# Up projection: a couple's second product added onto the bank of its first, and one weight split moved from GpSimd to VectorE

## The chip, the cores and the metric

The kernel runs on one core of a Trainium2 chip. The metric is the device time of one execution in microseconds (us), the median of several runs. The core has TensorE (PE in the rows; PEld is its loading of weights), VectorE (DVE), ScalarE (ACT), GpSimd (POOL) and SyncE (SP), which issues the transfers. Each engine executes its instructions in order and waits where a semaphore is not there yet.

## The reference

One layer of a bidirectional encoder on 2048 positions of width 1024, in float32: two token mixers, a merge, and a channel mixer. Only the channel mixer matters here:

```
h2 = _rmsnorm(x, norm2_g[l])
u = h2 @ ffn_up[l]
...
u = cw[0] * _shift_prev(u) + cw[1] * u + cw[2] * _shift_next(u) + ffn_conv_b[l]
u_gate, u_val = jnp.split(u, 2, axis=-1)
x = x + (jax.nn.silu(u_gate) * u_val) @ ffn_down[l]
```

## The kernel before

**Float32 from three products.** Each float32 operand is split into a high part (a cast by ScalarE, names ending in h) and a low part (source minus high, names ending in l; both in `split`, L226 and L227). A product is high·high, high·low and low·high, 4 blocks of the contraction each: 12 matmuls of 128x512 into one bank of TensorE's accumulator memory (PSUM).

**Seven products for eight.** The up projection, L1501 to L1680, works on pairs: one tile of 128 gate features (`ug`) and one of 128 value features (`uv`), over two blocks of 512 positions at a time. That is a 2x2 block product, done with Winograd's seven products: weights A11, S2, S3, S1, A12, A22, S4 against activations B11, T2, T3, T1, B21, T4, B22, in this order in `up_pair`. A11 and A12 are `whi`/`wlo`, S1 and S2 are `s1h`/`s1l`, S3 and A22 are `s3h`/`s3l`, S4 is `s4h`/`s4l`. So a pair is 84 matmuls, and the rows name a product by its activations: "mT3h,s3l" is the last third of S3·T3.

**What is made of the products.** The four results are `c11`, `c12` (halves of `ug`) and `c21`, `c22` (halves of `uv`). Before the change ScalarE copies the first product out of its bank (L1639), and seven additions by VectorE (`plus`, L1506) bring in the others; each product has a bank of its own, from a ring of eight (`bank`).

**The rest of a pair.** Two rows of weights are loaded by SyncE into `rw` (`raw_tile`, four buffers). GpSimd forms the sums (L1561), four additions a pair. ScalarE casts the high parts; the low parts are subtracted by GpSimd (`wlo`, `s3l`) and VectorE (`s1l`, `s4l`). The split weights S1, S3, S4 have one buffer each, so they are made anew as soon as the pair before is through with them. Then the convolution (`conv`): ScalarE makes the middle tap (L1605), VectorE adds the two others (L1606, L1607), twice for `ug` and twice for `uv`; ScalarE takes the SiLU (L1613), VectorE multiplies (L1615), SyncE writes the result out. GpSimd copies the edge columns (`halo`).

**Order.** There are two sweeps q of 21 pairs each, over the position blocks 1 and 2, then 0 and 3. At the turn between them all seven activation matrices are replaced (`load_mat`): half of each passes through one buffer, `wraw`, the next transfer into which waits for VectorE's subtraction from the last. A scheduler sets the order on each engine from priorities; `plus` has a raised one. Behind the second sweep a last tile of 128 mixed features and then the down projection (L1714 to L1716) follow.

Of the kernel before, what the change touches and what calls it, by code (L numbers as in the profile page):

```python
# [166 lines left out]
def _body(tc, A, out, dump=None, upto=99):  # L167
    nc = tc.nc
# [4 lines left out]
    def pool(stack, name, bufs=1, space=None, **kw):  # L173
        if space is None:
            return stack.enter_context(tc.tile_pool(name=name, bufs=bufs, **kw))
        return stack.enter_context(tc.tile_pool(name=name, bufs=bufs, space=space, **kw))
# [48 lines left out]
    def split(hi, lo, src, lo_eng=None, hi_eng=None):  # L225
        (hi_eng or nc.scalar.copy)(out=hi, in_=src)  # L226
        (lo_eng or nc.vector).tensor_tensor(out=lo, in0=src, in1=hi.bitcast(F32), op=ALU.subtract)  # L227
# [70 lines left out]
    def operand(b, q, **kw):  # L298
        t = [[q.tile([128, 4, BT], F32R, name=f"h{nm}{b}{i}", **kw) for nm in ("hi", "lo")] for i in range(2)]
        return [Halves([x[j] for x in t]) for j in range(2)]  # L300
# [3 lines left out]
    for b in range(NB):  # L304
        x_, y_ = operand(b, hb, **FOP) if b == NB - 1 else operand(b, hp)
# [93 lines left out]
    for b in range(NB):  # L399
        ps = pg.tile([128, 512], F32, name="pg", tag="pg")  # L400
# [3 lines left out]
        o = ev.tile([128, 512], F32, name="ev", tag="ev")  # L404
# [1015 lines left out]
    mats = {}  # L1420
# [77 lines left out]
    def prod(ps, *terms):  # L1498
        mm = [(w[ph == 2][:, k, :], x[ph == 1][:, k, :]) for w, x in terms for ph in range(3) for k in range(4)]
        for i, (w_, x_) in enumerate(mm):  # L1500
            nc.tensor.matmul(ps, w_, x_, start=i == 0, stop=i == len(mm) - 1)  # L1501
        return ps

    def plus(o, ps, t):
        with tc.high_priority(300):
            nc.vector.tensor_tensor(out=o, in0=ps, in1=t, op=ALU.add)  # L1506
# [29 lines left out]
    fw = pool(s6, "fw", reuse_waits="tile")  # L1536
# [6 lines left out]
    def raw_tile(src):  # L1543
        r = fr.tile([128, 8, 128], F32, name="rw", tag="rw", bufs=4)
        if src is not None:
            sync.dma_start(out=f2(r), in_=src)
        return r
# [10 lines left out]
    def pair_weights(i):  # L1558
        r1, r2 = raw_tile(A["wup"][2 * i]), raw_tile(A["wup"][2 * i + 1])
        a, b = slice(0, 4), slice(4, 8)  # L1560
        ps_ = lambda o, x, y, op: nc.gpsimd.tensor_tensor(out=o, in0=x, in1=y, op=op)  # L1561

        def parts(q, names, src, eng, n=8):
            h, l = [q.tile([128, n, 128], F32R, name=x, tag=x, bufs=2 if q is wp else 1) for x in names]
            split(f2(h), f2(l), f2(src), lo_eng=eng)
            return h, l

        h, l = parts(wp, ("whi", "wlo"), r1, nc.gpsimd)
        w = {"A11": (h[:, a], l[:, a]), "A12": (h[:, b], l[:, b])}
        rs = raw_tile(None)  # L1570
        ps_(rs[:, a], r2[:, a], r2[:, b], ALU.add)
        ps_(rs[:, b], rs[:, a], r1[:, a], ALU.subtract)
        h, l = parts(fw, ("s1h", "s1l"), rs, nc.vector)
        w["S1"], w["S2"] = (h[:, a], l[:, a]), (h[:, b], l[:, b])
        ps_(r2[:, a], r1[:, a], r2[:, a], ALU.subtract)
        h, l = parts(fw, ("s3h", "s3l"), r2, nc.gpsimd)
        w["S3"], w["A22"] = (h[:, a], l[:, a]), (h[:, b], l[:, b])
        ps_(r1[:, b], r1[:, b], rs[:, b], ALU.subtract)
        w["S4"] = parts(fw, ("s4h", "s4l"), r1[:, b], nc.vector, 4)
        return w  # L1580

    def bank():
        nbank[0] += 1
        return pus[(nbank[0] - 1) % 8 >= 3].tile([128, 512], F32, name="pu", tag="pu")
# [5 lines left out]
    def u_tile(q, m, tag):  # L1590
        u = fu.tile([128, 1030], F32, name=tag, tag=tag, bufs=2)
        if q == 1:
            nc.gpsimd.memset(u[:, 0:1], 0.0)
            nc.gpsimd.tensor_copy(out=u[:, 513:517], in_=halo[:, m, :])
            nc.gpsimd.memset(u[:, 1029:1030], 0.0)
        return u

    def u_done(q, m, u):
        if q == 0:
            nc.gpsimd.tensor_copy(out=halo[:, m, 0:2], in_=u[:, 2:4])  # L1600
            nc.gpsimd.tensor_copy(out=halo[:, m, 2:4], in_=u[:, 1024:1026])
# [8 lines left out]
    def glu(q, i, ug, uv):  # L1610
        for c0, n, t0 in SEG[q]:
            g = conv(2 * i, ug, c0, n)
            nc.scalar.activation(out=g, in_=g, func=AF.Silu)  # L1613
            v = conv(2 * i + 1, uv, c0, n)
            nc.vector.tensor_tensor(out=v, in0=v, in1=g, op=ALU.mult)  # L1615
            sync.dma_start(out=d_act[i, :, t0:t0 + n], in_=v)
# [11 lines left out]
    def up_pair(q, i, w, after):  # L1628
        ug, uv = u_tile(q, 2 * i, "ug"), u_tile(q, 2 * i + 1, "uv")
        c11, c12, c21, c22 = [u[:, c] for u in (ug, uv) for c in COLS[q]]  # L1630

        def pr(a, b):
            ps = prod(bank(), (w[a], mats[b]))
            after(b)
            return ps

        p1 = pr("A11", "B11")
        with tc.high_priority(300):
            nc.scalar.copy(out=c11, in_=p1)  # L1639
        plus(c12, pr("S2", "T2"), c11)  # L1640
        plus(c21, pr("S3", "T3"), c12)
        p5 = pr("S1", "T1")
        plus(c12, p5, c12)
        plus(c22, p5, c21)
        plus(c11, pr("A12", "B21"), c11)
        plus(c21, pr("A22", "T4"), c21)
        plus(c12, pr("S4", "B22"), c12)
        u_done(q, 2 * i, ug)
        u_done(q, 2 * i + 1, uv)
        return lambda: glu(q, i, ug, uv)  # L1650
# [9 lines left out]

    steps = [(0, 21)] + [(q, i) for q in range(2) for i in range(21)] + [(1, 21)]
    weights = lambda i: load_w(A["wup"][42]) if i == 21 else pair_weights(i)
    nw, pend = None, None
    for n, (q, i) in enumerate(steps):
        w = nw
        if n + 1 < len(steps):
            nw = weights(steps[n + 1][1])
        if n == 0:
            load_mat("T4", 7)
        turn = q == 0 and i == 20  # L1670
        if i == 21:
            fin = mixed(q, w)
        else:
            fin = up_pair(q, i, w, lambda b: load_mat(b, MATS.index(b)) if turn else None)
        if pend:
            pend()
        pend = fin
# [43 lines left out]
    def banks(tt):  # L1721
        return [pd.tile([128, 512], F32, name=f"pd{tt % 4}{i}", tag=f"pd{tt % 4}{i}") for i in range(2)]
# [59 lines left out]
    for w, (tt, k0) in enumerate(work):  # L1782
        ah, al = nx
        if k0 == 0:
            ps = banks(tt)
# [41 lines left out]
```

## Time and profile before

| | |
|---|---|
| median of 3 runs | 3567.59 us (3567.49 to 3571.24) |
| the profiled execution: its own time | 3570.72 us |
| its span, first to last instruction | 3568.9 us |
| TensorE busy | 3280.0 us, 92% |
| VectorE busy | 2328.1 us, 65% |
| ScalarE busy | 1571.5 us, 44% |
| GpSimd busy | 957.1 us, 27% |
| up projection, from its first to its last matmul | about 2200 to 3074 us |

The shares are averages over stages with different limits. Rows of the time line give the start, the duration, the engine, the line, what is written and what is read, the number of instructions, and in brackets how long the engine stood idle before and for whom.

### The profile page before, as it was taken

The numbers are of one execution on the slowest core, as the hardware profiler recorded it, in microseconds if no ns is written. First come the engines' busy times: TensorE is split into PE (matmuls) and PEld (weight loads), VectorE is DVE, ScalarE is ACT, GpSimd is POOL, SyncE is SP. The second block draws the span as 40 slices with busy tenths as digits, with TensorE's granted clock in tenths as the row PEclk, the third lists the DMA queues.
The fourth block names the chain that finished last, engine by engine and source line by source line (L and its number), as shares of the span: only waits on it lengthen the run. The fifth ranks groups of instructions, "written<-read, shape, count | busy, mean of one in ns | idle before, by whom it ended". The sixth has DMA issues, their size and how long they took to land.

```text
span 3568.9 us, 58167 instructions
## 1 busy us (share of the span) xinstructions
PE 3280.0 (92%) x22232; PEld 2612.0 (73%) x22232; DVE 2328.1 (65%) x3945; ACT 1571.5 (44%) x2870; POOL 957.1 (27%) x757
## 2 busy tenths in 40 slices
PE   7999999999978888888768999999989999999998
PEld 6787778766656766766656788877768777878887
DVE  5207664587865666666776467989899998723222
ACT  4214443455546776676544333344444434411111
POOL 1122222134440000000003314676676666100000
PEclk9999999999989999998889999999989999999999
DMA  4233443688874565556889656222232222523222
GB/s 148 93 118 107 132 137 129 193 225 228 230 227 152 161 188 155 181 181 195 238 241 340 220 160 197 83 77 80 80 130 89 81 79 77 177 81 114 84 84 62
DMA packets 403222, 531.29 MB, mean 149 GB/s; under 512 B 61504, under 2 KB 250560, under 8 KB 402944
## 3 DMA queue, kind: packets, MB, share of 16 engines
q1 hardware_dynamic: 402944, 527.58, 47.5%
q8 instruction: 175, 2.87, 0.3%
q14 instruction: 103, 0.84, 0.1%
HBM read 345.02 MB, written 181.93 MB: 148 GB/s over the span
## 4 chain that ended last, share of the span: by engine, by line
PE 32%; DVE 22%; issue 6%; DMA 6%; ACT 5%; POOL 1%; SPq 1%; DVEq 0%; ACTq 0%; POOLq 0%
PE pg L241 7%; PE pu L1501 6%; PE pd L1714 4%; PE pd L1715 4%; PE pd L1716 4%; DVE cv L1606 3%; PE pf L1218 2%; DVE ug L1506 2%; DVE s1l L227 2%; DVE uv L1506 2%; DVE tm L924 1%; DVE XX L925 1%; DMA d_m<-ev 1%; POOL s3l L227 1%; DVE cv L1607 1%
## 5 line engine op out<-in xcount | busy, mean ns | idle before, releaser
L227 POOL TENSOR_TENSOR wlo<-wraw,whi 128x1024 fp32r<-128x1024 f32 x46 | 115.2, 2504 | 1166.6 <-ACT whi L226 924.2
L1561 POOL TENSOR_TENSOR rw<-rw 128x512 f32<-128x512 f32 x168 | 274.5, 1653 | 4.4 <-DVE cv L1606 1.1
L1714 PE MATMUL pd<-wdh,whi 128*128 128x512 f32 x672 | 261.6, 391 | 1.3 <-DVE ug L1506 1.3
L1715 PE MATMUL pd<-wdl,whi 128*128 128x512 f32 x672 | 261.4, 389 | 0.0
L1716 PE MATMUL pd<-wdh,wlo 128*128 128x512 f32 x672 | 259.3, 389 | 0.0
L1218 PE MATMUL pf<-fop,whi 128*128 128x512 f32 x576 | 175.7, 442 | 87.4 <-ACT whi L226 59.4
L241 PE MATMUL pg<-hlo,whi 128*128 128x512 f32 x928 | 251.9, 404 | 0.0
L241 PE MATMUL pg<-hhi,whi 128*128 128x512 f32 x928 | 248.8, 403 | 3.1 <-ACT whi L226 3.1
L241 PE MATMUL pg<-hhi,wlo 128*128 128x512 f32 x928 | 247.2, 401 | 0.0
L241 PEld LDWEIGHTS pg<-hhi,whi 128*128 128x128 f32 x928 | 175.8, 192 | 55.8 <-issue 15.6
L241 PEld LDWEIGHTS pg<-hlo,whi 128*128 128x128 f32 x928 | 175.2, 192 | 52.7 <-issue 17.5
L241 PEld LDWEIGHTS pg<-hhi,wlo 128*128 128x128 f32 x928 | 175.1, 191 | 50.4 <-issue 14.7
L1218 PEld LDWEIGHTS pf<-fop,whi 128*128 128x128 f32 x576 | 112.7, 207 | 124.0 <-ACT whi L226 65.5
L1605 ACT ACTIVATE cv<-ug,vec 128x511 f32<-128x511 f32 (+1 forms) x88 | 71.9, 817 | 250.3 <-DVE ug L1506 250.3
L226 ACT CAST whi<-wraw 128x1024 fp32r<-128x1024 f32 x114 | 119.4, 1048 | 109.0 <-PE pg L241 53.7
L1703 ACT CAST whi<-wraw 128x1024 fp32r<-128x1024 f32 (+1 forms) x36 | 35.3, 980 | 265.8 <-PE pd L1715 185.9
L1606 DVE SCALAR_TENSOR_TENSOR cv<-ug,vec,cv 128x511 f32<-128x511 f32 (+1 forms) x88 | 125.4, 1425 | 36.8 <-ACT cv L1605 36.8
L1714 PEld LDWEIGHTS pd<-wdh,whi 128*128 128x128 f32 x672 | 126.1, 188 | 30.4 <-issue 4.7
L1716 PEld LDWEIGHTS pd<-wdh,wlo 128*128 128x128 f32 x672 | 126.1, 188 | 26.2
L1715 PEld LDWEIGHTS pd<-wdl,whi 128*128 128x128 f32 x672 | 126.1, 188 | 25.6
L1613 ACT ACTIVATE cv<-cv 128x511 f32<-128x511 f32 (+1 forms) x84 | 52.9, 630 | 198.4 <-DVE cv L1607 198.4
L1706 DVE TENSOR_TENSOR wlo<-wraw,whi 128x1024 fp32r<-128x1024 f32 (+1 forms) x36 | 39.3, 1092 | 150.5 <-ACT whi L1703 150.5
(470 smaller groups left out, 8230.4 us busy)
## 6 DMA issues: line engine op xcount, KB each, us to landing
rw<-wup SPq DMA_DIRECT2D x84, 512.0 KB, 3.5
wraw<-win SPq DMA_DIRECT2D x74, 512.0 KB, 4.2
Lt<-d_lt SPq DMA_DIRECT2D x64, 512.0 KB, 5.2
d_lt<-arbk SPq DMA_DIRECT2D x96, 256.0 KB, 3.9
d_gate<-ev SPq DMA_DIRECT2D x64, 256.0 KB, 3.6
X<-d_vt SPq DMA_DIRECT2D x64, 256.0 KB, 4.4
bj<-d_lt SPq DMA_DIRECT2D x128, 128.0 KB, 3.7
d_m<-ev SPq DMA_DIRECT2D x64, 256.0 KB, 5.1
```

The costliest lines, as they stand in the source:

```text
L226: (hi_eng or nc.scalar.copy)(out=hi, in_=src)
L227: (lo_eng or nc.vector).tensor_tensor(out=lo, in0=src, in1=hi.bitcast(F32), op=ALU.subtract)
L241: nc.tensor.matmul(ps, (wh, wh, wl)[ph], (xh, xl, xh)[ph], start=(ph == 0 and i == 0), stop=(ph == 2 and i == n - 1))
L1218: nc.tensor.matmul(ps, (wh, wh, wl)[ph][:, k0 + k, :], (hi, lo, hi)[ph][:, k, :], start=i == first[u] and k == 0, stop=i == last[u] and k ...
L1501: nc.tensor.matmul(ps, w_, x_, start=i == 0, stop=i == len(mm) - 1)
L1506: nc.vector.tensor_tensor(out=o, in0=ps, in1=t, op=ALU.add)
L1561: ps_ = lambda o, x, y, op: nc.gpsimd.tensor_tensor(out=o, in0=x, in1=y, op=op)
L1605: nc.scalar.activation(out=c, in_=u[:, c0:c0 + n], func=AF.Identity, scale=vc("cw1", m), bias=vc("cb", m))
L1606: nc.vector.scalar_tensor_tensor(out=c, in0=u[:, c0 - 1:c0 - 1 + n], scalar=vc("cw0", m), in1=c, op0=ALU.mult, op1=ALU.add)
L1714: nc.tensor.matmul(ps, a, wdh[k][:, cs], start=(k == 0), stop=False)
L1715: nc.tensor.matmul(ps, a, wdl[k][:, cs], start=False, stop=False)
L1716: nc.tensor.matmul(ps, l, wdh[k][:, cs], start=False, stop=False)
```

## The change

Three of the seven products are no longer put into a bank of their own. A12·B21 is added onto the bank of A11·B11, A22·T4 onto that of S3·T3, S4·B22 onto that of S1·T1, after the first product of the couple has been read out of it. So a pair takes four banks, VectorE makes five additions instead of seven, and ScalarE two copies (`taken`) instead of one. `s3l` goes from GpSimd to VectorE.

```diff
-        h, l = parts(fw, ("s3h", "s3l"), r2, nc.gpsimd)
+        h, l = parts(fw, ("s3h", "s3l"), r2, nc.vector)
...
-        def pr(a, b):
-            ps = prod(bank(), (w[a], mats[b]))
+        def pr(a, b, ps=None):
+            first = ps is None
+            ps = bank() if first else ps
+            mm = [(w[a][ph == 2][:, k, :], mats[b][ph == 1][:, k, :]) for ph in range(3) for k in range(4)]
+            for n, (w_, x_) in enumerate(mm):
+                nc.tensor.matmul(ps, w_, x_, start=first and n == 0, stop=n == len(mm) - 1, skip_group_check=True)
             after(b)
             return ps
+        def taken(o, ps):
+            with tc.high_priority(300):
+                nc.scalar.copy(out=o, in_=ps)
         p1 = pr("A11", "B11")
-        with tc.high_priority(300):
-            nc.scalar.copy(out=c11, in_=p1)
+        taken(c11, p1)
         plus(c12, pr("S2", "T2"), c11)
-        plus(c21, pr("S3", "T3"), c12)
+        p3 = pr("S3", "T3")
+        plus(c22, p3, c12)
         p5 = pr("S1", "T1")
-        plus(c12, p5, c12)
-        plus(c22, p5, c21)
-        plus(c11, pr("A12", "B21"), c11)
-        plus(c21, pr("A22", "T4"), c21)
-        plus(c12, pr("S4", "B22"), c12)
+        plus(c22, p5, c22)
+        taken(c11, pr("A12", "B21", p1))
+        plus(c21, pr("A22", "T4", p3), c12)
+        plus(c12, pr("S4", "B22", p5), c12)
```

The matmuls of a steady pair keep their order on TensorE. On VectorE, from the addition of S2·T2 in one pair of the first sweep on, this stood before (the additions in turn: S2·T2, S3·T3, S1·T1 twice, then behind `s1l` A12·B21, A22·T4, S4·B22):

```order
L1506 TENSOR_TENSOR ug<-pu,ug 128x512 [waits PE_49,Activation_49]
L1615 TENSOR_TENSOR cv<-cv 128x511 [waits DVE_49,Activation_49]
L1506 TENSOR_TENSOR uv<-pu,ug 128x512 [waits DVE_49,PE_49]
L1506 TENSOR_TENSOR ug<-pu,ug 128x512 [waits DVE_49,PE_49]
L1506 TENSOR_TENSOR uv<-pu,uv 128x512
L227 TENSOR_TENSOR s1l<-rw,s1h 128x1024 [waits Activation_49]
L1506 TENSOR_TENSOR ug<-pu,ug 128x512 [waits PE_49]
L1606 SCALAR_TENSOR_TENSOR cv<-ug,vec,cv 128x511 [waits Activation_49]
L1506 TENSOR_TENSOR uv<-pu,uv 128x512 [waits PE_49]
L1606 SCALAR_TENSOR_TENSOR cv<-uv,vec,cv 128x511 [waits DMAHW7_49,Activation_49]
L1607 SCALAR_TENSOR_TENSOR cv<-uv,vec,cv 128x511 [waits DVE_49]
L1506 TENSOR_TENSOR ug<-pu,ug 128x512 [waits PE_49]
```

And this stands there now (the additions: S2·T2, S3·T3, S1·T1, then A22·T4 and S4·B22):

```order
L1506 TENSOR_TENSOR ug<-pu,ug 128x512 [waits PE_49]
L1615 TENSOR_TENSOR cv<-cv 128x511 [waits DVE_49,Activation_49]
L1506 TENSOR_TENSOR uv<-pu,ug 128x512 [waits DVE_49,PE_49]
L1506 TENSOR_TENSOR uv<-pu,uv 128x512 [waits DVE_49,PE_49]
L227 TENSOR_TENSOR s1l<-rw,s1h 128x1024 [waits Activation_49]
L1606 SCALAR_TENSOR_TENSOR cv<-ug,vec,cv 128x511 [waits Activation_49]
L1506 TENSOR_TENSOR uv<-pu,ug 128x512 [waits PE_49]
L227 TENSOR_TENSOR s3l<-rw,s3h 128x1024 [waits DMAHW0_49,Activation_49]
L1606 SCALAR_TENSOR_TENSOR cv<-uv,vec,cv 128x511 [waits DMAHW7_49,Activation_49]
L1607 SCALAR_TENSOR_TENSOR cv<-uv,vec,cv 128x511 [waits DVE_49]
L1506 TENSOR_TENSOR ug<-pu,ug 128x512 [waits PE_49]
L227 TENSOR_TENSOR s4l<-rw,s4h 128x512 [waits DMAHW5_49,Activation_49]
```

One addition of S1·T1 and the one of A12·B21 are gone, and `s3l` has come in between the addition of A22·T4 and the convolution of `uv` that reads its result.

On ScalarE, from the middle tap of the second half on, this stood before (the COPY is the first product's):

```order
L1605 ACTIVATE cv<-ug,vec 128x511 [waits DVE_49,Activation_49]
L1605 ACTIVATE cv<-uv,vec 128x511 [waits DMAHW2_49]
L1613 ACTIVATE cv<-cv 128x511 [waits DVE_49]
L1639 COPY ug<-pu 128x512 [waits PE_49]
L1613 ACTIVATE cv<-cv 128x511 [waits DVE_49]
L226 CAST s1h<-rw 128x1024 [waits PE_49,Activation_49,Pool_49]
L226 CAST whi<-rw 128x1024 [waits DMAHW5_49,PE_49]
L1605 ACTIVATE cv<-ug,vec 128x511 [waits DVE_49]
L226 CAST s3h<-rw 128x1024 [waits PE_49,DMAHW4_49,Activation_49,Pool_49]
```

And this stands there now; behind `whi` the second COPY takes A11·B11 + A12·B21 out of the bank:

```order
L1605 ACTIVATE cv<-ug,vec 128x511 [waits DVE_49]
L1605 ACTIVATE cv<-uv,vec 128x511 [waits DMAHW2_49]
L1644 COPY ug<-pu 128x512 [waits PE_49]
L1613 ACTIVATE cv<-cv 128x511 [waits DVE_49] x2
L226 CAST s1h<-rw 128x1024 [waits PE_49,Pool_49]
L226 CAST whi<-rw 128x1024 [waits DMAHW5_49,PE_49]
L1644 COPY ug<-pu 128x512 [waits DVE_49,PE_49,Activation_49]
L1605 ACTIVATE cv<-ug,vec 128x511 [waits Activation_49]
L226 CAST s3h<-rw 128x1024 [waits DMAHW4_49,PE_49,Pool_49]
```

The middle tap of `ug` ahead of `s3h` waited for an addition of VectorE, and now waits for the copy on its own engine.

At the turn, on VectorE, between the splits of two matrices that pass through `wraw`, this stood before:

```order
L227 TENSOR_TENSOR mT3l<-wraw,mT3h 128x1024 [waits DMAHW4_49,Activation_49]
L227 TENSOR_TENSOR mT1l<-ev,mT1h 128x512 [waits DMAHW5_49,Activation_49]
L1506 TENSOR_TENSOR uv<-pu,uv 128x512 [waits DVE_49,PE_49]
L1606 SCALAR_TENSOR_TENSOR cv<-ug,vec,cv 128x511 [waits Activation_49]
L1506 TENSOR_TENSOR ug<-pu,ug 128x512 [waits PE_49]
L1606 SCALAR_TENSOR_TENSOR cv<-uv,vec,cv 128x511 [waits DMAHW3_49,Activation_49]
L227 TENSOR_TENSOR s4l<-rw,s4h 128x512 [waits DMAHW1_49,Activation_49]
L1607 SCALAR_TENSOR_TENSOR cv<-ug,vec,cv 128x511 [waits DVE_49]
L227 TENSOR_TENSOR mB21l<-ev,mB21h 128x512 [waits DMAHW0_49,Activation_49]
L1607 SCALAR_TENSOR_TENSOR cv<-uv,vec,cv 128x511 [waits DVE_49]
L1606 SCALAR_TENSOR_TENSOR cv<-ug,vec,cv 128x511 [waits Activation_49]
L227 TENSOR_TENSOR mT1l<-wraw,mT1h 128x1024 [waits DMAHW1_49,Activation_49]
```

And this stands there now:

```order
L227 TENSOR_TENSOR mT3l<-wraw,mT3h 128x1024 [waits DMAHW4_49,Activation_49]
L1606 SCALAR_TENSOR_TENSOR cv<-ug,vec,cv 128x511 [waits Activation_49]
L227 TENSOR_TENSOR mT1l<-ev,mT1h 128x512 [waits DMAHW5_49,Activation_49]
L1506 TENSOR_TENSOR uv<-pu,ug 128x512 [waits PE_49]
L227 TENSOR_TENSOR s3l<-rw,s3h 128x1024 [waits Activation_49]
L227 TENSOR_TENSOR mB21l<-ev,mB21h 128x512 [waits DMAHW0_49,Activation_49]
L1606 SCALAR_TENSOR_TENSOR cv<-uv,vec,cv 128x511 [waits DMAHW3_49,Activation_49]
L1506 TENSOR_TENSOR ug<-pu,ug 128x512 [waits PE_49]
L227 TENSOR_TENSOR s4l<-rw,s4h 128x512 [waits DMAHW1_49,Activation_49]
L227 TENSOR_TENSOR mT1l<-wraw,mT1h 128x1024 [waits DMAHW1_49,Activation_49]
```

Three passes of the convolution have gone behind `mT1l`, and `s3l` has come in ahead of it.

## Rows read from the trace of the kernel before

**Rows 1.** Busy time of each engine in two stretches: PE, PEld, DVE, ACT, POOL, PEclk, DMA.

```profile
2200.00:2300.00 100.00, 99.83 (x439) 82.38 (x440) 90.08 (x95) 44.17 (x60) 68.36 (x50) 1.00 0.39 125
2400.00:2500.00 100.00, 95.82 (x416) 76.94 (x415) 90.45 (x95) 40.56 (x55) 69.02 (x50) 1.00 0.24 79
```

**Rows 2.** Waits from 2300 to 2600 us: us in total, times, longest.

```profile
DVE cv L1606 <- ACT cv L1605: 26.5, 30, 0.9
...
PE pu L1501 <- POOL s3l L227: 12.6, 15, 0.9
```

**Rows 3.** Time line of TensorE: starts of pairs, and two places in one pair.

```profile
2238.18 1.07 PE L1501 MATMUL pu<-mB11h,whi 128*128 128x512 f32 x4
...
2257.22 1.07 PE L1501 MATMUL pu<-mB11h,whi 128*128 128x512 f32 x4
...
2316.04 1.07 PE L1501 MATMUL pu<-mB11h,whi 128*128 128x512 f32 x4
...
2324.39 1.19 PE L1501 MATMUL pu<-mT3h,s3l 128*128 128x512 f32 x4 [0.84 <-POOL s3l L227]
...
2330.87 1.07 PE L1501 MATMUL pu<-mT4h,s3h 128*128 128x512 f32 x4
...
2620.20 1.07 PE L1501 MATMUL pu<-mB11h,whi 128*128 128x512 f32 x4
...
2684.97 1.07 PE L1501 MATMUL pu<-mB11h,whi 128*128 128x512 f32 x4
...
2742.09 1.07 PE L1501 MATMUL pu<-mB11h,whi 128*128 128x512 f32 x4
...
3063.24 1.07 PE L1501 MATMUL pu<-mB11h,whi 128*128 128x512 f32 x4
```

**Rows 4.** Time line of VectorE in the pair from 2316.04 us on.

```profile
2317.78 1.22 DVE L227 TENSOR_TENSOR s1l<-rw,s1h 128x1024 fp32r<-128x1024 f32 x1
...
2320.48 1.47 DVE L1606 SCALAR_TENSOR_TENSOR cv<-ug,vec,cv 128x511 f32<-128x511 f32 x1 [0.88 <-ACT cv L1605]
...
2323.43 1.45 DVE L1606 SCALAR_TENSOR_TENSOR cv<-uv,vec,cv 128x511 f32<-128x511 f32 x1 [0.89 <-ACT cv L1605]
...
2328.50 1.78 DVE L1606 SCALAR_TENSOR_TENSOR cv<-ug,vec,cv 128x511 f32<-128x511 f32 x1
...
2334.21 0.74 DVE L1607 SCALAR_TENSOR_TENSOR cv<-uv,vec,cv 128x511 f32<-128x511 f32 x1
...
2336.07 0.68 DVE L1506 TENSOR_TENSOR uv<-pu,ug 128x512 f32<-128x512 f32 x1
```

**Rows 5.** Time line of ScalarE and GpSimd in the same pair.

```profile
2319.63 0.81 ACT L1605 ACTIVATE cv<-ug,vec 128x511 f32<-128x511 f32 x1 [3.68 <-DVE ug L1506]
...
2320.35 1.04 ACT L226 CAST s3h<-rw 128x1024 fp32r<-128x1024 f32 x1
...
2321.95 2.38 POOL L227 TENSOR_TENSOR s3l<-rw,s3h 128x1024 fp32r<-128x1024 f32 x1
...
2327.92 5.21 POOL L1561 TENSOR_TENSOR rw<-rw 128x512 f32<-128x512 f32 x3
...
2329.36 0.56 ACT L1639 COPY ug<-pu 128x512 f32<-128x512 f32 x1
```

**Rows 6.** GpSimd's sums beside a nearly idle VectorE; VectorE's additions from PSUM (min/median/max ns).

```profile
2189.72 5.15 POOL L1561 TENSOR_TENSOR rw<-rw 128x512 f32<-128x512 f32 x4
...
L1506 DVE TENSOR_TENSOR ug<-pu,ug x170: 674/680/694, 2205.8 to 3074.8; 128x512 f32<-128x512 f32 x170
```

**Rows 7.** Time lines of VectorE, ScalarE and TensorE at the turn.

```profile
2617.50 1.21 DVE L227 TENSOR_TENSOR mB11l<-wraw,mB11h 128x1024 fp32r<-128x1024 f32 x1
...
2645.15 2.28 DVE L227 TENSOR_TENSOR mT1l<-wraw,mT1h 128x1024 fp32r<-128x1024 f32 x1
...
2622.24 1.05 ACT L226 CAST mT2h<-wraw 128x1024 fp32r<-128x1024 f32 x1 [3.49 <-DMA wraw<-d_mat]
...
2647.48 2.07 PE L1501 MATMUL pu<-mT1l,s1h 128*128 128x512 f32 x4 [6.86 <-DVE mT1l L227]
```

## The prediction, as it was made before the change was timed

> **What bounds the kernel now.** I looked at the busy shares by stretch first, because the shares of the whole run say nothing about the one stage that the change touches. In the first 100 us of the up projection TensorE makes 439 matmuls, later 416 in 100 us, at the same granted clock of 1.00; VectorE is at 90% in both [rows 1]. So TensorE can go faster than it does, and something slows it from the fifth pair on. The time line of the pairs' starts says by how much: 19.04 us a pair at full rate (2238.18 to 2257.22), later 20.27 us, the mean of the 15 pairs from 2316.04 to 2620.20 [rows 3].
>
> The list of waits names a culprit: TensorE stands 0.84 us in every pair for GpSimd's `s3l` [rows 2, 3]. I don't believe that this is the whole cause. In the same list VectorE waits only for ScalarE, twice a pair (30 times in 15 pairs), and never for TensorE. Its time line in one pair shows why [rows 4]: it is late. TensorE starts A22·T4 at 2330.87, while VectorE adds S3·T3, finished some 5 us before that, only at 2336.07. VectorE works without a gap but for two waits of 0.88 and 0.89, in which ScalarE makes a middle tap (0.81 us) that had to wait for an addition of VectorE (3.68 us, [rows 5]). 90.45% of 20.27 us is 18.3 us of work, and 18.3 + 1.8 of these two waits makes 20.1 of the 20.27: VectorE's own chain, with its round trips to ScalarE, sets the period. `s3h` stands behind the middle tap on ScalarE [rows 5], so `s3l` is late because VectorE is. To move `s3l` alone would mend the symptom.
>
> **VectorE's work.** Two additions a pair go, at 0.68 us each [rows 4]: −1.36. One `s3l` comes: `s1l` has its shape and costs 1.22 [rows 4]: +1.22. By durations alone that is nothing: 7 additions (4.76), 8 passes of the convolution at 0.74 (5.92), 2 products (1.36, shaped like the additions), `s1l` 1.22 and `s4l` 0.68 make 13.94 before and 13.80 after. Measured are 18.3. The difference of 4.4 is stretching: a pass costs 0.74 alone and 1.78 where GpSimd's sums run beside it [rows 4, 5]. GpSimd's arithmetic in a pair is 5.15 for the four sums and 2.38 each for `wlo` and `s3l`, 9.9 in all [rows 5, 6]; 44% of it comes back as stretching. With `s3l` gone from GpSimd 7.5 remain, so at the same share 3.3: 17.1 us. The bounds are 13.8 (no stretching) and 21.3 (all 7.5 of it). I take 17.1, since the other instructions and what they meet stay as they are.
>
> **VectorE's two round trips.** The order on ScalarE removes the first: the tap of `ug` now waits for a copy on ScalarE itself (0.56), which waits only for TensorE. In the second, `s3l` now lies between the addition of A22·T4 and the pass on `uv`, 1.22 us of work against 0.89 of waiting. So VectorE's cycle falls from 20.27 to about 17.1, below TensorE's 19.04, and TensorE becomes the bound.
>
> **The new waits.** TensorE may add onto a bank only after its first product has been read. I laid the new order out from the rows, with A11·B11's start as zero and 2.72 us (19.04 / 7) a product. A12·B21 of the pair before ends at −5.4. ScalarE's copy (0.56) and tap (0.81) end at −4.0; VectorE's pass (1.47) at −2.5, by which time A22·T4 is through (−2.7); addition −1.9; `s3l` −0.6 (TensorE needs it at 7.3); four passes at 1.78, the addition of S4·B22 and `s4l` in between, end at 7.9; three passes and two products at their bare cost and the addition of S2·T2 at 12.1; S3·T3 read out at 12.8. A22·T4 may start at 13.6: 0.8 us to spare. S1·T1 is read out at 13.5, and S4·B22 starts at 16.3. Behind these two additions VectorE has only `s1l` of the next pair, needed at 23.6. The first product is copied right after ScalarE's two later taps, near 6, and A12·B21 starts at 10.9. Behind that copy stand, on ScalarE, the SiLU and the next pair's `s1h`, needed at 21.8. So the new waits cost nothing as long as VectorE's cycle stays below 19. ScalarE's added copy of 0.56 goes into an engine that is 41% busy [rows 1]. SyncE issues the same transfers in the same order; that of a new `rw` tile waits for `s1l` and `s4l`, which come earlier.
>
> **Gain of the steady pairs.** First sweep, 2238.18 to 2620.20: 19 pairs at 19.04 would take 361.8 instead of 382.0: 20.2. Second, 2742.09 to 3063.24: 16 pairs, 304.6 instead of 321.2: 16.5 [rows 3]. Together 36.7, less 1 for small waits.
>
> **The turn.** From 2620.20 to 2684.97 two pairs take 64.8 us instead of 38.1: 26.7 are lost to the new matrices [rows 3]. The chain through `wraw` begins with VectorE's `mB11l` at 2617.50, that is 17.6 us after the start of its pair (2.7 before the next, of 20.27); the transfer for T2 is what ScalarE then waits for [rows 7]. In the new layout VectorE comes to this place about 8 to 9 us after the pair's start, so the chain begins some 8 us earlier against TensorE. `mT1l`, for which TensorE stood 6.86 us [rows 7], moves ahead of three passes and behind one `s3l`: some 3 × 1.75 − 1.22 = 4 us. I take 12; the bounds are 0 (something else in the turn is late next, say ScalarE's casts) and 20 (all but what a chain of seven transfers must cost).
>
> **The start.** VectorE has the extra work of the mixed tile and of T4 in the first two pairs, and A22·T4 now waits for it there: −2 (bounds 0 and −5).
>
> **Sum:** 36.7 − 1 + 12 − 2 = 46 us. The profiled execution took 3570.7, 3.1 above the median; 3570.7 − 46 = 3525, and beside the runs timed, 3567.6 − 46 = 3522.
>
> **Weighed against the skill.** The row first: a pass costs 0.74 alone and 1.78 beside GpSimd's sums, while an addition that reads PSUM never leaves 674 to 694 ns in 170 cases [rows 4, 6]. The Trainium skill, "SBUF — State Buffer", section "Who interferes with whom", says that VectorE and GpSimd share a port, and that a VectorE instruction with two inputs in SBUF and a GpSimd instruction that reads SBUF shut each other out for the whole instruction. The trace agrees in kind. It speaks against the half of the change that gives VectorE another such instruction, and by it all of GpSimd's 7.5 us could stand in VectorE's way: the case of 21.3 us, the second rival below.
>
> **Rivals.**
> 1. The pairs reach 19.04, but the turn does not shorten, or grows a little: gain 36.7 − 1 − 2 = 34, down to 25 if the new order makes the turn 9 worse: 3533 to 3543. For it: seven transfers still go through one buffer. Against it: VectorE, which was late there, is early.
> 2. VectorE stays the bound, and it becomes slower. The place is A22·T4, which now waits for the addition of S3·T3: TensorE, with no spare banks to run ahead in, follows VectorE's cycle. It decides from a stretching of 20.27 − 13.80 = 6.5 of GpSimd's 7.5 us on (86%, against 44% now). At 21.3 us a pair the 32 steady pairs lose 1.0 to 1.2 each, 36, and some seven pairs that ran at 19.04 lose 2.3 each, 16: 52 us more, 3620. Against it: the additions never stretch, so GpSimd has VectorE's 3.4 us of them to run beside.
> 3. In between: stretching of 70 to 86% or a wait at A22·T4 puts the pairs at 19.4 to 20.1: gain 5 to 25, 3543 to 3562.
> 4. TensorE's wait for `s3l` was all there was to win, 0.84 in some 34 pairs, and another wait comes in its place: a gain near 0, 3565.
>
> **How the numbers follow.** The forecast, pairs at TensorE's rate and a shorter turn, gets 0.66; its own range is 3508 to 3532 (turn 0 to 20, start 0 to −5). Rival 1 gets 0.17, rival 3 0.08, rival 4 0.04, rival 2 0.05. The range from 3508 to 3541 takes in the forecast and most of rival 1. A change of 0.2%, 7 us, is about what a measurement of this kernel can tell from none. The forecast, rival 1 and rival 3 (nearly all of it) are faster: 0.91; the same 0.04; slower 0.05.
>
> **What would show it.** Pairs start every 19.04 to 19.1 us in both sweeps; in the middle of a sweep TensorE waits neither for `s3l` nor for an addition or copy; VectorE is busy 86 to 92% of the pair, its passes ahead of `uv` no longer wait for ScalarE, and it waits now and then for TensorE. B11's row two pairs behind the turn comes 45 to 60 us after the turn's, not 64.8. It is wrong if a wait of TensorE for L1506 ahead of "mT4h,s3h" appears in every pair, if `s3l` on VectorE runs 2 us or more, or if the turn is as long as before.

## The result, and the profile after

The changed kernel took 3534.48 us in the median, the kernel before 3569.41 beside it. The four executions of the changed kernel took 3531.80, 3532.77, 3536.19 and 5318.39 us, and the last, at a granted clock of 0.555, counts in that median but not in the comparison (the median of the other three is 3532.77). The ratio is 0.9895, with a 95% interval of 0.9877 to 0.9913: a gain of about 37.5 us, where 46 were forecast. The profiled execution took 3531.80, its span is 3530.0, against 3570.72 and 3568.9 before.

First the busy time by stretch, in the columns of [rows 1]:

```profile
2200.00:2220.00 20.00, 17.16 (x77) 13.98 (x76) 14.95 (x19) 12.13 (x19) 10.96 (x8) 0.91 0.73 217
...
2400.00:2500.00 100.00, 100.00 (x443) 82.81 (x442) 89.97 (x95) 47.63 (x64) 67.22 (x48) 1.00 0.25 85
2800.00:2900.00 100.00, 100.00 (x443) 82.81 (x442) 90.97 (x94) 45.57 (x61) 54.35 (x58) 1.00 0.26 85
```

TensorE makes 443 matmuls in 100 us in the middle of either sweep, where 416 were made before, and never stands still. VectorE's share is 90% as before: but 90% of a pair of 19.04 us, not of 20.27. So it works 17.1 us a pair instead of 18.3. The share of an engine alone would have hidden the change; its product with the period shows it.

The list of waits from 2300 to 2580 us, columns as in [rows 2]:

```profile
DVE cv L1606 <- ACT cv L1605: 25.8, 14, 1.9
```

No wait of TensorE is left in it, and VectorE's wait for ScalarE comes once a pair instead of twice. It is also a different wait, as VectorE's time line in one pair shows, to be read against [rows 4]:

```profile
2351.86 1.22 DVE L227 TENSOR_TENSOR s1l<-rw,s1h 128x1024 fp32r<-128x1024 f32 x1
2354.94 1.66 DVE L1606 SCALAR_TENSOR_TENSOR cv<-ug,vec,cv 128x511 f32<-128x511 f32 x1 [1.86 <-ACT cv L1605]
2356.52 0.68 DVE L1506 TENSOR_TENSOR uv<-pu,ug 128x512 f32<-128x512 f32 x1
2357.12 1.21 DVE L227 TENSOR_TENSOR s3l<-rw,s3h 128x1024 fp32r<-128x1024 f32 x1
2358.25 0.74 DVE L1606 SCALAR_TENSOR_TENSOR cv<-uv,vec,cv 128x511 f32<-128x511 f32 x1
```

and ScalarE's in the same pair, against [rows 5]:

```profile
2352.52 1.06 ACT L226 CAST whi<-rw 128x1024 fp32r<-128x1024 f32 x1 [1.61 <-PE pu L1638]
2353.48 0.58 ACT L1644 COPY ug<-pu 128x512 f32<-128x512 f32 x1
2354.09 0.82 ACT L1605 ACTIVATE cv<-ug,vec 128x511 f32<-128x511 f32 x1
```

The pass on `ug` waits for the tap, the tap for the copy, and the copy stands behind the cast of `whi`, for which ScalarE had waited 1.61 us for TensorE; TensorE's last row of A12·B21 ends at about the time at which the copy starts (2352.32 + 1.07, and 2353.48). VectorE waits for TensorE, in effect: 1.86 us a pair is the room that it has. The pass on `uv` no longer waits; `s3l` stands where it waited before.

Last, TensorE's time line, against [rows 3] and [rows 7]: the first two rows of the stage, the starts of pairs 4, 5 and 20 of the first sweep, the turn, pair 4 and the mixed tile of the second sweep, and the first row of the down projection.

```profile
2204.64 1.21 PE L1638 MATMUL pu<-mB11h,whi 128*128 128x512 f32 x4 [2.84 <-DVE wraw L1506]
2205.65 1.91 PE L1638 MATMUL pu<-mB11l,whi 128*128 128x512 f32 x4
...
2282.50 1.07 PE L1638 MATMUL pu<-mB11h,whi 128*128 128x512 f32 x4
...
2301.54 1.07 PE L1638 MATMUL pu<-mB11h,whi 128*128 128x512 f32 x4
...
2587.14 1.07 PE L1638 MATMUL pu<-mB11h,whi 128*128 128x512 f32 x4
...
2621.28 1.44 PE L1638 MATMUL pu<-mT1l,s1h 128*128 128x512 f32 x4 [3.83 <-DVE mT1l L227]
...
2657.62 1.20 PE L1638 MATMUL pu<-mT4h,s3h 128*128 128x512 f32 x4 [0.72 <-DVE uv L1506]
...
2676.53 1.98 PE L1638 MATMUL pu<-mT4h,s3h 128*128 128x512 f32 x4 [2.41 <-DVE uv L1506]
2678.30 1.90 PE L1638 MATMUL pu<-mT4l,s3h 128*128 128x512 f32 x4
...
2695.91 1.20 PE L1638 MATMUL pu<-mT4h,s3h 128*128 128x512 f32 x4 [0.69 <-DVE uv L1506]
...
2701.48 1.07 PE L1638 MATMUL pu<-mB11h,whi 128*128 128x512 f32 x4
...
3025.16 1.07 PE L1501 MATMUL pu<-mB11h,whi 128*128 128x512 f32 x4
3037.07 0.47 PE L1722 MATMUL pd<-wdh,whi 128*128 128x512 f32 x1 [0.88 <-DVE ug L1506]
```

From 2301.54 to 2587.14 fifteen pairs take 19.04 each, and from 2701.48 to 3025.16 seventeen. Between 2587.14 and 2701.48 five pairs take 114.3 us; at full rate it would be 95.2. These 19.1 us are the loss at the turn. In it the new wait shows, that of A22·T4 for VectorE to read S3·T3 out of the bank, in the three pairs behind the turn; behind the longest, 2.41 us of standing, TensorE's rows take 1.98 and 1.90 instead of 1.07: the granted clock is 0.52 from 2676.53 to 2680.00, for most of it the lower of its two levels (1.2 instead of 2.4 GHz).

**The account.** The stage, from its first matmul to the first of the down projection, took 875.6 us before (2200.01 to 3075.61) and 832.4 after: 43.2 less. Of these, 36.7 are the steady pairs and 7.6 the turn (26.7 to 19.1, as counted in the prediction); 0.5 come at the end, where the last wait is 0.88 instead of 1.33; 1.6 are lost at the start. The rest of the program is the same code, but the stage began 4.6 us later (2204.64 for 2200.01) and ended 0.4 us nearer to the end of the program. 43.2 − 4.6 + 0.4 is about the 38.9 between the two spans.

### The profile page after: what moved, and what is told of

The parts are those of the page before. It is cut to its first block, busy times and chain, and to the rows that moved or that the text cites. A ratio compares the mean times of both kernels' runs of the same rounds, so it can differ in the third digit from the quotient of the medians.

```text
span 3530.0 us, 58016 instructions
## 1 busy us (share of the span) xinstructions
PE 3282.4 (93%) x22232; PEld 2626.9 (74%) x22232; DVE 2281.4 (65%) x3903; ACT 1609.0 (46%) x2912; POOL 875.7 (25%) x715
## 4 chain that ended last, share of the span: by engine, by line
PE 48%; DVE 12%; DMA 6%; ACT 4%; issue 2%; SPq 1%; POOL 0%; DVEq 0%; ACTq 0%; POOLq 0%
PE pu L1638 20%; PE pg L241 6%; PE pd L1722 4%; PE pd L1724 4%; PE pd L1723 4%; PE pf L1218 3%; DVE tm L924 1%; DVE XX L925 1%; DMA d_m<-ev 1%; DMA wraw<-win 1%; DVE X L1027 1%; DVE gX L1004 1%; DVE wlo L227 1%; ACT TT L938 1%; DMA ev<-d_gate 1%
## 5 line engine op out<-in xcount | busy, mean ns | idle before, releaser
L1561 POOL TENSOR_TENSOR rw<-rw 128x512 f32<-128x512 f32 x168 | 282.1, 1694 | 72.4 <-DVE s3l L227 59.7
L227 DVE TENSOR_TENSOR wlo<-wraw,whi 128x1024 fp32r<-128x1024 f32 x68 | 84.1, 1237 | 79.3 <-ACT whi L226 79.2
```

## The experiments

In each, the stage and the turn say more than the time of the whole. Each line of the table is read from one profiled execution, though, and the executions of one kernel spread over 3 to 16 us, so that a few us in its last column are not shown to be the edit's. The ends of the stage are the same two rows of TensorE as above. The loss at the turn is what the 22 pairs from the last of the first sweep to the mixed tile take beyond 22 × 19.04 (for the kernel before, whose steady pairs are slower, as in the prediction).

| kernel | stage from, to | stage, us | loss at the turn, us |
|---|---|---|---|
| before | 2200.01, 3075.61 | 875.6 | 26.7 |
| changed | 2204.64, 3037.07 | 832.4 | 19.1 |
| own bank for A22·T4 | 2213.36, 3044.69 | 831.3 | 18.0 |
| two buffers at the turn | 2202.56, 3037.82 | 835.3 | 22.7 |
| last quarters to VectorE | 2207.31, 3036.18 | 828.9 | 14.4 |
| `wlo` to VectorE | 2200.03, 3027.67 | 827.6 | 15.4 |
| both to VectorE | 2200.70, 3021.23 | 820.5 | 8.8 |
| both, and own bank | 2201.31, 3031.75 | 830.4 | 18.2 |

**One half of the change alone: `s3l`.** The kernel before with

```diff
-        h, l = parts(fw, ("s3h", "s3l"), r2, nc.gpsimd)
+        h, l = parts(fw, ("s3h", "s3l"), r2, nc.vector)
```

> Kernel before with one edit: s3l made by VectorE; seven banks, seven additions and one copy stay. Theory (VectorE's chain sets the pair): its work goes from 18.3 to about 18.3 - 1.05 (44% of GpSimd's 2.38) + 1.22 = 18.5 us, the wait for the tap of uv is covered by s3l, that for the tap of ug (0.88) stays: 19.4 us a pair, TensorE still waits a little for s3l, and the stage gains some 27 of the 37 us of its steady pairs. Rival (s3l alone made TensorE late): pairs at exactly 19.04, a gain of 37 or more. Other rival (VectorE has no room for another 1.22): pairs stay at 20.1 to 20.3, gain under 5.

3542.59 us, ratio 0.9924 (0.9909 to 0.9939). The stage took 842.5 us (2206.55 to 3049.07), 33.1 less than before. The pairs of the first sweep started every 19.04 us; in the second they slowed to 19.69 from the tenth on. Busy time in a stretch of either sweep, and a row of TensorE in the second:

```profile
2400.00:2500.00 100.00, 100.00 (x442) 82.78 (x442) 94.48 (x106) 42.56 (x57) 66.61 (x49) 1.00 0.25 81
...
2860.00:2960.00 100.00, 98.67 (x429) 79.38 (x428) 94.85 (x102) 41.07 (x55) 51.50 (x56) 1.00 0.24 79
```

```profile
2847.46 1.20 PE L1501 MATMUL pu<-mT3h,s3l 128*128 128x512 f32 x4 [0.26 <-DVE s3l L227]
```

VectorE works 94.48% of 19.04, 18.0 us, and waits 0.89 once a pair: 18.9, just under TensorE's 19.04. In the second sweep it is 94.85% of 19.69 and the same wait: 19.6, over it, and TensorE waits again. This half is worth more than I had given it: VectorE's work fell by 0.3 us although it got 1.22 more. The 19.04 of the first sweep is also what the rival gave, so this run alone does not decide between the two; for VectorE's chain speaks the second sweep, where TensorE waits again with `s3l` on VectorE, and the next run.

**The other half alone: the banks.** The changed kernel with `s3l` back on GpSimd.

```diff
-        h, l = parts(fw, ("s3h", "s3l"), r2, nc.vector)
+        h, l = parts(fw, ("s3h", "s3l"), r2, nc.gpsimd)
```

> Changed kernel with one edit undone: s3l made by GpSimd again; four banks, five additions and two copies stay. Theory: VectorE's work is 18.3 - 1.36 = 16.9 us, one round trip of 0.89 stays: 17.8 us, under TensorE's 19.04. s3h no longer stands behind a tap that waits for VectorE, so s3l comes in time: pairs at 19.04, the gain of the whole change, about 38 to 45 us, and the turn no longer than with it. Rival (GpSimd is too slow for s3l): TensorE waits for s3l 0.5 to 0.9 in every pair, pairs at 19.6 to 19.9, gain 10 to 20.

3546.72 us, ratio 0.9933 (0.9918 to 0.9947); stage 842.8 us (2209.52 to 3052.33), 32.8 less than before. TensorE waits for `s3l` no more although GpSimd makes it, which speaks against the rival, here and in the run before. But the pairs of the first sweep take 19.26 in the mean (16 from 2287.49 to 2595.62 us), not 19.04: in about one of three, A22·T4 waits for its bank. TensorE's rows, the second one behind the turn:

```profile
2397.55 1.20 PE L1638 MATMUL pu<-mT4h,s3h 128*128 128x512 f32 x4 [0.33 <-DVE uv L1506]
...
2688.37 1.19 PE L1638 MATMUL pu<-mT4h,s3h 128*128 128x512 f32 x4 [2.60 <-DVE uv L1506]
```

VectorE works 17.6 us a pair by its busy share from 2400 to 2500 us (91.44% of 19.26), and 17.9 over fourteen whole pairs, where it was 18.3 and 18.4 before: 0.4 to 0.7 less, where two additions of 0.68 are gone. The halves gain 33.1 and 32.8 alone and 43.2 together: both mend the same lateness, and TensorE's rate is the floor.

**More additions on VectorE.** Two more in every pair of the changed kernel, and four in the next (range(4)):

```diff
-        plus(c12, pr("S4", "B22", p5), c12)
+        p7 = pr("S4", "B22", p5)
+        plus(c12, p7, c12)
+        for _ in range(2):
+            plus(jk, p7, c12)
```

> Changed kernel with two more additions of 0.68 on VectorE in every pair (the last product of the pair added again, into a tile that nobody reads). Theory: VectorE stands 1.86 us in a steady pair for the tap behind TensorE's A12.B21; 1.36 fit in: pairs stay at 19.04 and that wait falls to 0.5, the time grows by under 6 us, at the two ends of the sweeps. Rival (VectorE is still tied to the period): each addition costs its 0.68, pairs at 20.4, 45 us more than the changed kernel.

> The same with four more additions, 2.72 us. Theory: 1.86 fit in, 0.86 don't: pairs at 19.9 us, TensorE waits in every pair for VectorE ahead of A22.T4 or for s3l, some 30 us more than the changed kernel, a little under the kernel before. Rival (VectorE has more room than its wait shows, since the additions do not stretch and take stretching off others): pairs at 19.04 to 19.4.

With two, 3531.45 us, ratio 0.9890 (0.9875 to 0.9905): as fast as the changed kernel. With four, 3558.21, ratio 0.9962 (0.9949 to 0.9974). And the four again, with both inputs in SBUF:

```diff
+        for _ in range(4):
+            plus(jk, c12, c12)
```

> Changed kernel with four more additions on VectorE in every pair, as in the run with four before, but both inputs in SBUF (c12 + c12) instead of one in PSUM. Theory (an addition from PSUM gives GpSimd a place to run, one from SBUF takes a place): 17.1 + 2.72 = 19.8, and the wait of 1.86 in which GpSimd ran is gone, so up to 1.9 more stretching: pairs at 19.8 to 21.7 in the first sweep, against 19.34 with the four from PSUM. Rival (where the inputs lie makes no difference): 19.34 in the first sweep, 20.0 in the second, as there.

3587.87 us, ratio 1.0047 (1.0031 to 1.0063). The busy time from 2400 to 2500 us in the three:

```profile
2400.00:2500.00 100.00, 100.00 (x443) 82.84 (x442) 90.00 (x107) 48.28 (x64) 67.89 (x49) 1.00 0.26 85
```

```profile
2400.00:2500.00 100.00, 99.79 (x434) 80.74 (x433) 99.82 (x116) 46.36 (x61) 58.69 (x47) 1.00 0.27 83
```

```profile
2400.00:2500.00 100.00, 96.79 (x421) 78.44 (x420) 99.82 (x111) 44.22 (x60) 68.47 (x45) 1.00 0.26 79
```

The first row is the surprise. VectorE has 1.36 us more to do, and its share stays at 90.00%: by the list of waits it still waits 26.4 us in 15 pairs. What the two additions take, the other instructions no longer lose to stretching. In the second sweep that is not so: there its share rises from 91% to 99%; why that sweep has less room was not tried. With four, VectorE is never idle, and pairs take 19.36 in the first sweep (2357.90 to 2551.53, ten pairs), as the rival gave, and 20.0 in the second, as the theory gave. With inputs in SBUF alone it is 20.0 and 20.7, as the theory gave: the same number of instructions of the same bare length, in nearly the same places of VectorE's order, costs some 0.65 us a pair more, and GpSimd's arithmetic takes 11.4 us a pair instead of 8.7. So it counts where the inputs lie.

**More work on GpSimd.** The changed kernel, where GpSimd makes `wlo` twice:

```diff
         h, l = parts(wp, ("whi", "wlo"), r1, nc.gpsimd)
+        for _ in range(1):
+            for c in (a, b):
+                nc.gpsimd.tensor_tensor(out=f2(jk), in0=f2(r1[:, c]), in1=f2(h[:, c]).bitcast(F32), op=ALU.subtract)
```

> Changed kernel with GpSimd making wlo a second time in every pair (two subtractions of 128x512, some 2.4 us, into a tile that nobody reads). By the prediction's price, 44% of GpSimd's time comes back on VectorE: its share in the first sweep goes from 89.9% to about 95% (+1.05 us), pairs stay at 19.04, time the same. Rival, from the runs with more additions: GpSimd runs freely only beside VectorE's additions from PSUM (3.4 us) and its wait (1.86), and these are taken by the 7.5 us it has: all 2.4 come back, 17.1 + 2.4 = 19.5 us: VectorE at 99% and pairs at 19.2 to 19.6, 5 to 15 us more.

3577.31 us, ratio 1.0014 (1.0003 to 1.0025): the whole gain is gone, from some 2.4 us more a pair on an engine that is busy 67% of the time. Busy time and TensorE's waits from 2300 to 2580:

```profile
2400.00:2500.00 100.00, 96.21 (x420) 77.99 (x419) 96.65 (x90) 45.30 (x60) 80.74 (x55) 1.00 0.24 79
```

```profile
PE pu L1642 <- DVE uv L1506: 10.4, 14, 0.8
```

Pairs take 20.1 in both sweeps. VectorE works 96.65% of that, 19.4 us: 2.3 more than in the changed kernel, of GpSimd's 2.4. The rival's price holds, not the 44%; its 19.2 to 19.6 for the pairs was still too little, since VectorE also waits some 0.5 us in every pair for A22·T4 itself. And TensorE waits 0.74 in every pair at A22·T4: the place that the prediction's second rival named is where the change breaks when VectorE is late.

**The new wait at the turn.** A22·T4 in a bank of its own:

```diff
-        plus(c22, p3, c12)
+        plus(c21, p3, c12)
...
-        plus(c22, p5, c22)
+        plus(c22, p5, c21)
...
-        plus(c21, pr("A22", "T4", p3), c12)
+        plus(c21, pr("A22", "T4"), c21)
```

> Changed kernel with A22.T4 in a bank of its own again: c21 = S3.T3 + c12, c22 = S1.T1 + c21, c21 = A22.T4 + c21, so still five additions and two copies, five banks a pair. Theory: adding A22.T4 onto the bank of S3.T3 saves no addition, and only makes TensorE wait for VectorE behind the turn (0.72 + 2.41 + 0.69 us, and some 1.7 at the lower clock behind the longest): pairs at 19.04, these waits gone, the stage 2 to 6 us shorter than the 832.4 of the changed kernel. Rival (VectorE is late there with or without the bank, and the wait moves to s1l, s3l or the ring of banks): 830 to 834.

3531.84 us, ratio 0.9886 (0.9869 to 0.9904). The bank waits are gone and the loss at the turn is 18.0 instead of 19.1: the rival. TensorE's waits there now:

```profile
2631.35 2.07 PE L1638 MATMUL pu<-mT1l,s1h 128*128 128x512 f32 x4 [4.74 <-DVE mT1l L227]
...
2641.25 2.08 PE L1638 MATMUL pu<-mB21l,whi 128*128 128x512 f32 x4 [3.52 <-DVE mB21l L227]
```

**The buffer at the turn.** Two transfers of 128x512 through two buffers, instead of one of 128x1024 through `wraw`:

```diff
-        r = wp.tile([128, 1024], F32, name="wraw", tag="wraw", bufs=1)
...
+        for k in range(4):
+            if k == 0:
+                r = wp.tile([128, 1024], F32, name="wraw", tag="wraw", bufs=1)[:, 0:BT]
+            elif k == 1:
+                r = fc.tile([128, BT], F32, name="mq")
...
```

> Changed kernel, where the first half of each activation matrix no longer passes through wraw in one transfer of 128x1024, but in two of 128x512, one through wraw and one through a buffer of its own. Theory (the turn is the chain transfer, cast, subtraction, seven times over, through one buffer): a step falls from about 3.8 + 1.05 + 1.2 to some 3.3 + 0.6 + 0.7, so the seven become some 8 to 11 us shorter, and the loss at the turn falls from 19.1 to 8 to 13 us. Rival (VectorE's work at the turn sets it): 17 to 20.

3530.30 us, ratio 0.9886 (0.9872 to 0.9900), but the turn lost 22.7, more than before the edit: my theory of the turn fell. Rows of VectorE and of TensorE:

```profile
2621.70 0.68 DVE L227 TENSOR_TENSOR mT1l<-mq,mT1h 128x512 fp32r<-128x512 f32 x1
```

```profile
2622.43 1.65 PE L1640 MATMUL pu<-mT1l,s1h 128*128 128x512 f32 x3 [3.84 <-DVE mT1l L227]
...
2694.31 2.08 PE L1640 MATMUL pu<-mT4h,s3h 128*128 128x512 f32 x4 [3.34 <-DVE uv L1506]
```

The cast of that part was through at 2616.43, and VectorE, without a gap, came to its subtraction only at 2621.70. For this matrix it is VectorE's list that is late, not the transfer.

**Work taken off GpSimd.** If its time and VectorE's add up, what GpSimd does slowly should be cheaper on VectorE. First the last quarter of each matrix at the turn, then `wlo` in every pair, then both with and without the own bank:

```diff
-            split(mats[n][0][:, k, :], mats[n][1][:, k, :], r, lo_eng=nc.gpsimd if k == 3 else nc.vector)
+            split(mats[n][0][:, k, :], mats[n][1][:, k, :], r, lo_eng=nc.vector)
...
-        h, l = parts(wp, ("whi", "wlo"), r1, nc.gpsimd)
+        h, l = parts(wp, ("whi", "wlo"), r1, nc.vector)
```

> Changed kernel; of each activation matrix that is loaded at the turn, the low part of the last quarter (128x512) is made by VectorE instead of GpSimd (0.68 us bare, instead of 1.3 to 2.0 on GpSimd). Theory (at the turn VectorE's instructions with both inputs in SBUF and GpSimd's take turns, so what counts there is the sum of both): seven times some 0.9 us less, the loss at the turn falls from 19.1 to 12 to 16 us, the stage from 832.4 to 826 to 830. Rival (only VectorE's own list counts there): seven times 0.68 more, the loss grows to 21 to 25 us.

3530.60 us, ratio 0.9882 (0.9862 to 0.9902); the loss at the turn is 14.4, within what the theory gave.

> Changed kernel with wlo made by VectorE too; GpSimd keeps the four sums. VectorE's bare work in a pair goes from 13.80 to 15.02 us, GpSimd's from 7.5 to 5.15. Theory (GpSimd's time comes back one for one, less what runs beside additions and waits): VectorE's share of a steady pair of the first sweep falls a little or stays, 84 to 90%, though it has 1.22 us more to do; pairs at 19.04; the turn 2 to 5 us shorter. By the prediction's price of 44%: 15.02 + 2.3 = 17.3 us, 91%. Rival (VectorE's list is what counts): share 94% and more, waits of TensorE at A22.T4 or for wlo, and a longer turn.

3528.86 us, ratio 0.9873 (0.9855 to 0.9890), loss at the turn 15.4, shorter as expected. From 2400 to 2500 us:

```profile
2400.00:2500.00 100.00, 100.00 (x443) 82.81 (x442) 91.29 (x101) 47.67 (x62) 53.13 (x41) 1.00 0.25 84
```

VectorE's share is 91.3%, which the 44% gave and the theory of one for one did not: of GpSimd's 2.4 us that are gone, VectorE got back only 0.9.

> Changed kernel with three edits together: wlo and the last quarters at the turn on VectorE, and A22.T4 in a bank of its own. Theory: pairs at 19.04 with more room, the turn shorter by 6 to 10 us (loss 9 to 13), the stage 822 to 827 and the time 6 to 10 us under that of the changed kernel. Rival: the turn waits for T1l and B21l whatever VectorE has to do, stage 829 to 833.

3526.20 us, ratio 0.9869 (0.9853 to 0.9885), loss at the turn 18.2: the rival, and the worst of the three.

> Changed kernel with wlo and the last quarters at the turn on VectorE, A22.T4 added onto the bank of S3.T3 as in the changed kernel: it differs from the run with three edits by this bank alone. If the two moves off GpSimd add up (4.7 and 3.7 us at the turn), the loss at the turn is 10 to 13 us, the stage 823 to 826, the time some 6 to 9 us under that of the changed kernel. If they pay for the same wait, the loss stays at 14 to 16 us and the stage at 827 to 829. If it is as with the own bank (18.2 us, 830), the bank is not what spoiled that run.

3522.92 us, ratio 0.9862 (0.9844 to 0.9881); stage 820.5, loss at the turn 8.8. The two moves add up and a little more, and the edit of the bank was what spoiled the stage of the run before. TensorE's rows of `mT1l` without the own bank, and with it:

```profile
2613.16 1.20 PE L1638 MATMUL pu<-mT1l,s1h 128*128 128x512 f32 x4 [0.87 <-DVE mT1l L227]
```

```profile
2616.25 2.08 PE L1638 MATMUL pu<-mT1l,s1h 128*128 128x512 f32 x4 [3.72 <-DVE mT1l L227]
```

In both kernels the turn's pair had started 31.5 and 33.5 us before. With the own bank, VectorE's order at the turn is another one, and `mT1l` comes 2 us later. That this order, and not the bank itself, makes the 9 us was not tried apart. The kernel with both moves has the lowest median of all here: its four executions took 3516.3 to 3524.2, the lowest three of the changed kernel 3531.8 to 3536.2. By the ratios and their intervals it is not told apart from the two runs before it; its stage is 7 to 10 us shorter than theirs.

## Why the prediction was right, point by point

The time, 3534, lies in the range, 2 us beyond the forecast's own (3508 to 3532) and within that of the first rival (3533 to 3543). That own range was added up wrongly: with the turn at 0 to 20 and the start at 0 to −5, 36.7 − 1 gives gains of 30.7 to 55.7, so 3512 to 3537, and the time lies in it. The rows decide between the two: the pairs reached 19.04 and the turn did get shorter, which is the forecast. Most of what is missing from the 46 us is the turn (4.4 us less than put) and a stage that began 4.6 us later than in the profile of before, which no term held.

**The bound.** VectorE's chain, not TensorE's wait for `s3l`, sets the pair. `s3l` alone and the banks alone each shortened VectorE's cycle and with it the pair; four additions more, or 2.4 us more on GpSimd, lengthened both again. What I said against moving `s3l` alone ("would mend the symptom") was wrong: it gains 33 of the 43 us.

**VectorE's 17.1 us.** 89.97% of 19.04 is 17.1: as forecast, but out of errors that nearly cancel. The two additions alone were worth 0.4 to 0.7 and not 1.36; `s3l` alone was worth −0.3 and not +0.17, since more of GpSimd's 2.38 had come back on VectorE than 44%. The step that failed is the fixed share of 44%.

Its size was wrong as well. The prediction set the durations of VectorE's rows, added end to end, against its busy time, but the rows overlap: in the pair above the addition at 2356.52 takes 0.68, and the next row starts at 2357.12. Over thirteen whole pairs the rows of before add up to 19.6 us, of which 18.4 are busy time, so the stretching was 5.6 and not 4.4. The changed kernel overlaps by the same 1.2, so the forecast did not feel it. In the table the rows of whole pairs of the first sweep are added up, and what they take beyond their bare durations (0.68, 0.74 and 1.22) is the stretching; the share is that of GpSimd's bare arithmetic.

| kernel | GpSimd, bare, us a pair | VectorE's rows | bare | stretching | share |
|---|---|---|---|---|---|
| before | 9.9 | 19.6 | 13.9 | 5.6 | 57% |
| `s3l` alone | 7.5 | 19.4 | 15.2 | 4.2 | 56% |
| banks alone | 9.9 | 19.0 | 12.6 | 6.4 | 64% |
| changed | 7.5 | 18.2 | 13.8 | 4.4 | 58% |
| two additions more | 7.5 | 18.4 | 15.2 | 3.2 | 43% |
| four more | 7.5 | 21.0 | 16.5 | 4.5 | 59% |
| four more, from SBUF | 7.5 | 21.6 | 16.5 | 5.1 | 68% |
| `wlo` made twice | 9.9 | 20.6 | 13.8 | 6.8 | 69% |
| `wlo` on VectorE | 5.2 | 18.6 | 15.0 | 3.5 | 68% |

The share is lowest where VectorE has two more additions from PSUM and still waits, and highest where VectorE got more work from SBUF (four additions, `wlo`) or GpSimd more of its own (`wlo` twice); this is read from the rows, and no run tried it apart. The additions from PSUM themselves stretch in none of these kernels (less than 0.05 us a pair). The Trainium skill, "SBUF — State Buffer", section "Who interferes with whom", says that a VectorE instruction with at most one input in SBUF does not contend with GpSimd (outside certain modes that use two ports), and that one with two inputs in SBUF contends with a GpSimd instruction that reads SBUF. By it the additions from PSUM leave GpSimd free to run and those from SBUF do not: the runs with four of each agree (19.36 against 20.0 us a pair).

How GpSimd can shut VectorE out shows ahead of the stage, in the kernel before, at a VectorE multiplication of two single columns in SBUF, alone and beside GpSimd:

```profile
2186.82 0.16 DVE L253 TENSOR_TENSOR n2t<-n2t,n2v 128x1 f32<-128x1 f32 x1
...
2187.41 2.37 DVE L253 TENSOR_TENSOR n2t<-n2t,n2v 128x1 f32<-128x1 f32 x1
...
2187.37 2.39 POOL L227 TENSOR_TENSOR wlo<-rw,whi 128x1024 fp32r<-128x1024 f32 x1 [11.42 <-ACT whi L226]
```

Begun 0.04 us behind GpSimd's subtraction, it takes 2.37 instead of 0.16 and ends with it. This suggests that what GpSimd costs VectorE depends on which instruction VectorE has in hand when GpSimd begins, and that no one share can stand for it: of 2.4 us more on GpSimd 2.3 came back (`wlo` made twice), of 2.4 us less only 0.9 (`wlo` on VectorE).

**The steady pairs.** 19.04 in both sweeps, and no wait of TensorE between: 36.7, as worked out, without the 1 us for small waits.

**The new waits.** None in the steady pairs. The 0.8 us to spare at A22·T4 were too few: the addition of S3·T3 ends 11.5 us after the start of its pair and not 12.8, and 2.1 are left (rows of VectorE and TensorE in the pair that starts at 2339.62):

```profile
2350.47 0.68 DVE L1506 TENSOR_TENSOR uv<-pu,ug 128x512 f32<-128x512 f32 x1
...
2353.22 1.07 PE L1638 MATMUL pu<-mT4h,s3h 128*128 128x512 f32 x4
```

The place was right: with 2.4 more on GpSimd TensorE waits just there. The adding of A22·T4 onto S3·T3's bank saves no addition, which I had not seen: with an own bank there are still five.

**The turn: the term that was mis-sized.** 12 us were forecast (bounds 0 and 20), 7.6 came. The chain did begin earlier: `mB11l` 8.4 us after the start of its pair instead of 17.6, and TensorE waited 3.83 for `mT1l` instead of 6.86. But the waits for the bank in the three pairs behind the turn, 3.8 us, and the lower clock after them took part of it back. Of the 26.7 us lost before, TensorE stood 15.9, and the other 10.8 went into rows that took longer (granted clock 0.79 from 2620.20 to 2684.97); of the 19.1 in the changed kernel it stood 12.4 (0.97 from 2587.14 to 2701.48).

I had taken the turn for a chain of transfers. With two buffers the loss was 22.7, with the own bank 18.0: neither of them is what the changed kernel waits for there. Taking work off GpSimd shortened it by 4.7, 3.7 and, both together, 10.3 us. But with the own bank the same two moves shortened nothing (18.0 to 18.2). So the work that VectorE and GpSimd have at the turn counts, and the order in which VectorE comes to it seems to count as much; that order was not tried apart, and the cause of the turn's length stays open in part.

**The start.** 1.6 us were lost, near the 2 that I had put, but not to VectorE: TensorE does not wait. In the first 20 us its granted clock is 0.91 where it was 1.00 before, after the same 2.84 us of standing. That is not shown to come from the change: of the ten kernels here that stood those 2.84 us, the clock fell in six and stayed at 1.00 in four, in no order that goes with the edits.

**What the sum did not hold.** The stage began 4.6 us later than in the profile of before. In the fourteen kernels it began between 2200.0 and 2213.4 us, in no order that goes with the edits; the code ahead of it is the same. The time of this program is uncertain by that much, and it is most of why the gain by the spans, 38.9, is less than the stage's 43.2.

## What to carry to other kernels

A busy share says nothing until it is multiplied by the period; an engine that is 90% busy before and after can have become 1.2 us shorter a step. Where VectorE and GpSimd both work from SBUF, count them together: here `s3l` and `wlo` were cheaper on the engine that does them faster, although that one is the busier, and removing two additions from PSUM gave back less than their duration. Adding a product onto a bank saved work where it saved an addition; where it saved none, it brought a wait of 0.69 to 2.41 us behind the turn, though the kernels without it were not shown to be faster.

## What the runs showed of the hardware

Two VectorE additions of 0.68 us from PSUM cost nothing in the first sweep (share 89.97% and 90.00%), and all of their time in the second (91% and 99%). Some 2.4 us more a pair on GpSimd, which was idle a third of the time, cost 43 us in all (3534.5 to 3577.3). Behind a wait of 2.84 us, TensorE's granted clock fell in the changed kernel (0.91 in the first 20 us, rows of 1.91 and 1.86 where 1.07 is usual) and did not in the kernel before (1.00); at the turn it fell behind a wait of 2.41 us too (0.52 in the 3.5 us behind it).
